# Stick-breaking attention with weights and values in two parts, both parts of the values in one stationary operand, a PSUM bank a head

## The chip, the core and the metric

The kernel runs on one core of a Trainium2 chip. A core has five engines that work side by side and follow one another through semaphores: TensorE (PE: the matmuls; PEld is its loading of stationary operands), VectorE (DVE), ScalarE (ACT), GpSimd (POOL) and SyncE (SP, which issues transfers). The metric is the device time of one execution in microseconds (us); lower is better.

## The reference, cut to what matters

Two transformer blocks run one after the other on one sequence of 512 positions with 1024 features, in fp32. The second block mixes three attentions, and the change is in one of them, stick-breaking attention, which has 8 heads of 64 features:

```
z = einsum('bqhd,bkhd->bhqk', q_b, bk) * HEAD_DIM ** -0.5
causal = kpos[None, :] < qpos[:, None]
log_beta = log_sigmoid(z)
log_one_minus = where(causal, log_sigmoid(-z), 0.0)
tail = cumsum(log_one_minus, reverse=True) - log_one_minus
a = where(causal, exp(log_beta + tail), 0.0)
return einsum('bhqk,bkhd->bqhd', a, bv)
```

Its result goes through a matrix (`@ w_up_b`) and is weighted with a gate, `merged = gates_a * ya + gates_b * yb + gates_c * yc`, where each gate is the sigmoid of a projection with a bias.

## The kernel before, in words

All activations lie with the features on the 128 partitions and the 512 positions along the free dimension. The large matrix products are made in fp32r, a format in which one pass does not carry all of fp32's digits; so each operand is held as a high and a low part, and each product takes three matmuls (high by high, low by high, high by low). Weights come by DMA as fp32; ACT rounds them to the high part `whi` (L358) and DVE subtracts to get the low part `wlo` (L359). The main matmuls (L231) accumulate one tile of 128 features by 512 positions in one of three PSUM banks, named `pd`; an evacuation on DVE or ACT frees the bank.

Small work runs as Python generators beside that stream. `start(gen, rate)` hangs a generator in, and after every so many main matmuls `pump` lets it take a step; `finish(gen)` runs what is left of it at once. The order in each engine's queue is then set by priorities when the program is built. A generator of stages goes through `pipeline`: in step i it issues stage 0 of unit i, stage 1 of unit i-1 and stage 2 of unit i-2.

Stick-breaking attention is the generator `stick`. It has 32 units: a pair of heads c = 0 to 3, a block of 128 keys kt = 3, 2, 1, 0, and a head hh = 0, 1 of the pair. Since a query sees only earlier keys, a unit has N = 512 - 128 kt queries: 128, 256, 384 and 512 columns. A unit does:
- stage 0: q·k into a PSUM bank `ps` of four (L584, L585), a mask by a small matmul (L1152), then on ACT abs (L180), exp and log(1 + x) (both L177), on DVE the softplus (L1158), which for kt < 3 is split in parts `P` by ACT (L547) and DVE (L548);
- stage 1: the running sums are added into `ps` by matmuls with triangular and all-ones matrices (L1169 in fp32 at kt = 3, L1172, L1177), while POOL keeps the sums of the key blocks passed so far (L1182 to L1190); ACT then takes the exponential of `ps` into a tile `PT` (L177), one of five such tiles;
- stage 2: the weights times the values. When the second head of a block comes to it, two fp32 matmuls (L1206) are issued, one a head, each with 64 stationary columns, for the upper and the lower 64 partitions of one bank `po`. That bank was cleared by a matmul with zeros at the pair's start (L1200), and ACT copies it out at the pair's end (L1210). The profile shows each fp32 matmul of L1206 as two instructions.

q·k and the triangular matmuls are made at least 256 columns wide or, at kt = 3, in fp32.

Beside `stick` runs `gated`, for the gate and the matrix of memory attention: for each half, four gate tiles (evacuated to `H` by DVE, L749), then one group of four sigmoids on ACT (`act_group`, L186, with a load of the activation tables ahead of it and another ahead of the next exponential), then four tiles of the matrix, whose evacuation multiplies with the sigmoids (DVE, L763). Then `finish(g_sb)` ends `stick`, and the next stage makes tiles of keys and queries in turn (evacuations L1670 and L1631 on DVE). At the start of `stick`, the top-256 search of another attention (`topk`, L1078 and L1079) still runs on DVE.

```python
        self.start(g_sb, 2.8)
        merged = self.t("H16", [P, KD, S])
        bg = lambda b: (lambda j: 8 * b + j)
        self.gated("gc", "uc", bg(2), u, R, yc, merged, True)
        self.finish(g_sb)
```

Of the kernel before, what the change touches and what calls it, by code (L numbers as in the profile page):

```python
# [8 lines left out]
F32 = mybir.dt.float32  # L9
F32R = mybir.dt.float32r  # L10
BF16 = mybir.dt.bfloat16
AF = mybir.ActivationFunctionType
# [5 lines left out]
P = 128  # L18
S = 512
D = 1024  # L20
KD = D // P
NT = S // P
# [115 lines left out]
NPT = 5  # L138
# [8 lines left out]
class Build:  # L147
# [82 lines left out]
    def mm(self, *args, **kw):  # L230
        return self.pe(self.nc.tensor.matmul(*args, **kw))  # L231
# [163 lines left out]
    def fm_tile(self, ws, rhs_hi, rhs_lo, cols):  # L395
        N = cols.stop - cols.start
        ps = self.bk_d()[:, 0:N]
        mm = self.mm
        for k, (hi, lo) in enumerate(ws):
            xh, xl = rhs_hi(k)[:, cols], rhs_lo(k)[:, cols]  # L400
            mm(ps, hi, xh, start=(k == 0), stop=False)
            mm(ps, hi, xl, start=False, stop=False)
            mm(ps, lo, xh, start=False, stop=(k == len(ws) - 1))
            self.pump(N / 4096.0)
        return ps

    def fm(self, name, rhs_hi, rhs_lo, evac, N=S):

        ps = self.fm_tile(self.next_half(name), rhs_hi, rhs_lo, slice(0, N))
        self.done_tile(lambda: evac(ps))  # L410
# [33 lines left out]
    def seven(self, name, x, pairs, evac):  # L444

        nc = self.nc

        def product(ps, b, start=False):  # L450
            hi, lo = x[b]
            kw = dict(skip_group_check=True)
            for k, (wh, wl) in enumerate(self.next_half(name)):
                self.mm(ps, wh, hi(k), start=start and k == 0, stop=False, **kw)
                self.mm(ps, wh, lo(k), start=False, stop=False, **kw)
                self.mm(ps, wl, hi(k), start=False, stop=k == 3, **kw)

        def head(q):
            q["g0"], q["c0"] = self.bk_s()[:, 0:256], self.bk_d()[:, 0:256]
            q["g1"] = self.seeded[:, 256 * (q["j"] % 2):256 * (q["j"] % 2) + 256]  # L460
            q["u2"], q["u4"] = self.t("s7", [P, 256], F32, bufs=2), self.t("s7b", [P, 256], F32, bufs=1)
            product(q["g0"], "11", True)

        def seed(q):
            nc.scalar.copy(q["g1"], q["g0"])

        def mid(q):
            product(q["c0"], "t3", True)
            product(q["g1"], "t2")
            nc.scalar.copy(q["u2"], q["g1"])  # L470
            product(q["g0"], "21")
            product(q["g1"], "t1")
            nc.scalar.copy(q["u4"], q["g1"])
            q["lin"] = self.tmp()
            nc.vector.tensor_add(q["lin"][:, 256:512], q["u4"], q["c0"])

        def tail(q, between):
            product(q["g1"], "22")
            between()
            gate = evac[0](q["g0"], q["g1"])  # L480
            product(q["c0"], "t4")
            nc.vector.tensor_add(q["lin"][:, 0:256], q["u2"], q["c0"])  # L482
            evac[1](q["j"], gate, q["lin"])
            self.done_tile(lambda: None)

        self.strict = "start"
        last = None
        for j in pairs:
            q = dict(j=j)
            head(q)  # L490
            if last is None:
                seed(q)
            else:
                tail(last, lambda: seed(q))
            mid(q)
            last = q
        if last is not None:
            tail(last, lambda: None)
        self.strict = None
# [284 lines left out]

    def softmax_finish(self, Pt, sums, N):
        nc = self.nc
        r = self.sm(1)
        nc.vector.reciprocal(r, sums)
        nc.vector.tensor_scalar(Pt[:, :N], Pt[:, :N], r, None, op0=ALU.mult)
# [348 lines left out]
    def stick(self, bk, bqh, bql, bv, y):  # L1138
        nc = self.nc
        units = [dict(c=c, kt=kt, hh=hh) for c in range(4) for kt in (3, 2, 1, 0) for hh in range(2)]  # L1140
        A, Ah, Al, o = {}, {}, {}, {}
        low = self.t("M4", [P, 2, 384], F32R)

        def s0(u):
            c, kt, h = u["c"], u["kt"], 2 * u["c"] + u["hh"]
            N = S - P * kt
            W = max(N, 256)
            z = self.bk_s()
            self.qk(z[:, :W], bk(h)[:, kt * P:(kt + 1) * P], bqh(h)[:, S - W:], bql(h)[:, S - W:])
            z = u["z"] = z[:, W - N:]  # L1150

            nc.tensor.matmul(z[:, :P], self.identb, self.strictb, start=False, stop=True, skip_group_check=True)  # L1152
            sp = u["sp"] = self.tmp()
            a = sp[:, :N]
            self.act(a, z[:, :N], AF.Abs)
            self.act(a, a, AF.Exp, scale=-1.0)
            self.act(a, a, AF.Ln, bias=self.ones[:, 0:1])
            nc.vector.scalar_tensor_tensor(a, z[:, :N], 0.0, a, op0=ALU.max, op1=ALU.add)  # L1158
            if kt < 3:
                hi = u["hi"] = self.t("P", [P, S], F32R, bufs=5)  # L1160
                lo = u["lo"] = self.t("P", [P, S], F32R, bufs=5)
                self.split_to(hi[:, :N], lo[:, :N], a)

        def s1(u):
            c, kt, h = u["c"], u["kt"], 2 * u["c"] + u["hh"]
            N = S - P * kt
            z, sp = u["z"], u["sp"]
            if kt == 3:
                nc.tensor.matmul(z[:, :N], self.ntri, sp[:, :N], start=False, stop=True, skip_group_check=True)  # L1169
            else:  # L1170
                for part in (u["hi"], u["lo"]):
                    nc.tensor.matmul(z[:, :N], self.ntrir, part[:, :N], start=False, stop=True,  # L1172
                                     skip_group_check=True)
                n = N - P
                parts = [Ah[h][:, 0:n], Al[h][:, 0:n]] if kt < 2 else [A[h][:, 3 * P:]]
                for part in parts:
                    nc.tensor.matmul(z[:, P:N], self.nones if kt < 2 else self.nones.bitcast(F32), part,  # L1177
                                     start=False, stop=True, skip_group_check=True)
            if kt == 3:
                A[h] = self.t("A", [P, S], F32, bufs=2)  # L1180
            if kt > 0:
                nc.gpsimd.tensor_copy(A[h][:, kt * P:(kt + 1) * P], sp[:, :P])  # L1182
                if kt < 3:
                    r = A[h][:, (kt + 1) * P:]
                    nc.gpsimd.tensor_add(r, r, sp[:, P:N])
                    Ah[h] = self.t("T", [P, S], F32R, bufs=2)
                    Al[h] = low[:, u["hh"], :]
                    a = A[h][:, kt * P:]
                    nc.gpsimd.tensor_copy(Ah[h][:, 0:N], a)
                    nc.gpsimd.tensor_sub(Al[h][:, 0:N], a, Ah[h][:, 0:N].bitcast(F32))  # L1190
            a = u["a"] = self.t("PT", [P, S], F32, bufs=NPT)
            self.act(a[:, :N], z[:, :N], AF.Exp)

        def s2(u):
            c, kt = u["c"], u["kt"]
            if u["hh"] == 0:
                return
            if kt == 3:
                o[c] = self.bk_o()
                nc.tensor.matmul(o[c], self.zb, self.zb[:, None, :].to_broadcast([P, 4, P]),  # L1200
                                 start=True, stop=True)
            us = [units[units.index(u) - 1], u]
            N = S - P * kt
            for hh in range(2):
                h = 2 * c + hh
                nc.tensor.matmul(o[c][64 * hh:64 * hh + 64, kt * P:], bv[:, kt, h * 64:(h + 1) * 64],  # L1206
                                 us[hh]["a"][:, :N], start=False, stop=True, skip_group_check=True)
            if kt == 0:
                y.append(self.t("Y", [P, S], F32, bufs=4))
                nc.scalar.copy(y[c], o[c])  # L1210

        yield from self.pipeline(units, [s0, s1, s2])

    def memattn(self, cq, mk, mv, y):
# [658 lines left out]
```

## Time and profile before

| | |
|---|---|
| time, median of 3 runs | 1727.21 us (1726.84 to 1728.08) |
| the profiled execution's own time | 1726.64 us |
| its span in the trace | 1724.9 us |
| PE matmuls busy | 1696.0 us, 98% of the span |
| PE weight loads busy | 1459.9 us, 85% |
| DVE busy | 1197.8 us, 69% |
| ACT busy | 916.4 us, 53% |
| POOL busy | 180.1 us, 10% |

The profile was taken on one execution. "Busy" counts the time in which an engine has an instruction in work; PE's matmuls overlap one another, so that a matmul's cost on PE is read from the start of one to the start of the next, and not from its own duration.

### The profile page before, as it was taken

How to read it: one execution, taken by the hardware profiler on the slowest of the kernel's cores; microseconds unless marked ns; L12 is line 12 of the kernel's file. 1: busy time of each engine (PE TensorE's matmuls, PEld its weight loads, DVE VectorE, ACT ScalarE, POOL GpSimd, SP SyncE). 2: the span in 40 equal slices, each digit the busy share in tenths (PEclk: the TensorE clock that was granted, in tenths of full speed). 3: DMA queues.
4: the chain of work that ended last, by engine and by line, in shares of the span. 5: the costliest groups of instructions: out<-in, count | busy, mean ns of one | idle time of the engine just before them, and what ended most of it. 6: DMA issues, size and time to landing. Idle time of an engine off the chain costs nothing. (4 is left out here: it accounts for less than half of the span.)

```text
span 1724.9 us, 27517 instructions
## 1 busy us (share of the span) xinstructions
PE 1696.0 (98%) x10178; PEld 1459.9 (85%) x10178; DVE 1197.8 (69%) x2515; ACT 916.4 (53%) x1875; POOL 180.1 (10%) x235
## 2 busy tenths in 40 slices
PE   8999999999999999999999999999999989999997
PEld 8878788888998989988989776777779979898997
DVE  5887765657866858886599944766655776585865
ACT  5755565545643635664455567644445454463542
POOL 1400001000100101000000223100001500010101
PEclk9999999999999999999999999999999999999999
DMA  5433215442655736245224111423233635474622
GB/s 180 123 90 122 77 59 150 132 141 91 161 152 128 186 114 159 73 132 170 86 78 106 62 62 61 116 82 117 66 120 103 162 85 145 125 183 117 156 75 82
DMA packets 74887, 199.75 MB, mean 116 GB/s; under 512 B 8864, under 2 KB 11464, under 8 KB 74496
## 3 DMA queue, kind: packets, MB, share of 16 engines
q1 hardware_dynamic: 64064, 178.53, 33.7%
q0 software_dynamic: 10688, 19.47, 6.9%
q8 instruction: 80, 1.31, 0.3%
q14 instruction: 55, 0.45, 0.1%
HBM read 187.45 MB, written 6.84 MB: 113 GB/s over the span
## 5 line engine op out<-in xcount | busy, mean ns | idle before, releaser
L358 ACT CAST whi<-raw 128x512 fp32r<-128x512 f32 (+2 forms) x504 | 288.3, 580 | 410.2 <-PE pd L231 269.3
L359 DVE TENSOR_TENSOR wlo<-raw,whi 128x512 fp32r<-128x512 f32 (+2 forms) x504 | 324.9, 650 | 204.8 <-ACT whi L358 198.8
L231 PE MATMUL pd<-uh,whi 128*128 128x512 f32 (+1 forms) x776 | 305.1, 393 | 0.0
L231 PE MATMUL pd<-uh,wlo 128*128 128x512 f32 (+1 forms) x776 | 304.5, 392 | 0.0
L231 PE MATMUL pd<-ul,whi 128*128 128x512 f32 (+1 forms) x776 | 303.5, 391 | 0.0
L231 PEld LDWEIGHTS pd<-uh,wlo 128*128 128x128 f32 x776 | 145.8, 188 | 33.9 <-issue 3.3
L231 PEld LDWEIGHTS pd<-ul,whi 128*128 128x128 f32 x776 | 145.9, 188 | 30.1 <-issue 1.7
L231 PEld LDWEIGHTS pd<-uh,whi 128*128 128x128 f32 x776 | 145.9, 188 | 29.8 <-issue 2.2
L231 PE MATMUL pd<-Yl,whi 128*128 128x256 f32 (+1 forms) x340 | 114.3, 336 | 3.8 <-ACT Yl L434 3.8
L231 PE MATMUL pd<-Yh,whi 128*128 128x256 f32 (+1 forms) x340 | 114.3, 339 | 0.9 <-DVE H L763 0.9
L231 PE MATMUL pd<-Yh,wlo 128*128 128x256 f32 (+1 forms) x340 | 114.0, 335 | 0.0
L231 PE MATMUL pd<-Ba,whi 128*128 128x512 f32 (+1 forms) x240 | 91.8, 383 | 1.2 <-DVE tmp L482 1.2
L231 PE MATMUL pd<-Ba,wlo 128*128 128x512 f32 (+1 forms) x240 | 90.9, 379 | 0.0
L231 PE MATMUL pd<-Ca,whi 128*128 128x512 f32 (+1 forms) x240 | 90.8, 378 | 0.0
L231 PE MATMUL ps<-ul,whi 128*128 128x256 f32 x296 | 83.2, 281 | 0.0
L231 PE MATMUL ps<-uh,wlo 128*128 128x256 f32 x296 | 83.1, 281 | 0.0
L231 PE MATMUL ps<-uh,whi 128*128 128x256 f32 x296 | 83.0, 281 | 0.0
L231 PE MATMUL pd<-Cb,whi 128*128 128x512 f32 (+1 forms) x210 | 79.8, 380 | 0.0
L231 PE MATMUL pd<-Bb,wlo 128*128 128x512 f32 (+1 forms) x210 | 79.6, 379 | 0.0
L231 PE MATMUL pd<-Bb,whi 128*128 128x512 f32 (+1 forms) x210 | 77.8, 380 | 1.4 <-ACT Bb L547 1.4
L358 ACT CAST whi<-PT 128x512 fp32r<-128x512 f32 x74 | 46.0, 621 | 58.9 <-PE po L231 25.1
L231 PEld LDWEIGHTS pd<-Yl,whi 128*128 128x128 f32 x340 | 64.2, 189 | 10.5 <-ACT Yl L434 4.1
(531 smaller groups left out, 4338.8 us busy)
## 6 DMA issues: line engine op xcount, KB each, us to landing
raw<-in_wts SPq DMA_DIRECT2D x202, 512.0 KB, 3.6
PT<-in_wts SPq DMA_DIRECT2D x74, 256.0 KB, 3.8
PT<-in_wts POOLq DMA_DIRECT2D x74, 256.0 KB, 5.1
raw<-in_wts SPq DMA_DIRECT2D x32, 448.0 KB, 3.4
P<-in_wts SPq DMA_DIRECT2D x37, 256.0 KB, 3.5
raw<-in_wts SPq DMA_DIRECT2D x8, 520.0 KB, 3.5
tabd<-tab SPq DMA_DIRECT2D x8, 320.0 KB, 5.8
H<-in_xT SPq DMA_DIRECT2D x8, 256.0 KB, 5.8
```

The source lines that it names most:

```text
L231: return self.pe(self.nc.tensor.matmul(*args, **kw))
L358: self.nc.scalar.copy(hi, r)
L359: self.nc.vector.tensor_sub(lo, r, hi.bitcast(F32))
```

## The change

For each unit the weights are split in a high and a low part (DVE, L1203 and L1204), which takes three `PT` tiles where there was one. For each pair of heads a new function `values` splits the values likewise (ACT L1147, DVE L1148) and lays them out so that a head's 64 high and 64 low columns stand side by side, as 128 stationary columns. Stage 2 then issues two fp32r matmuls a unit (L1213), one for each part of the weights, in the unit's own step. Their result has the products with the high values on one half of the partitions and those with the low values on the other; head 0 has the bank `po`, head 1 takes a bank `ps`. The matmul with zeros is gone. At a pair's end each head's two halves are added: ACT copies one half to SBUF (L1220), and DVE adds the other (L1221). Two scratch tiles of another function take other buffers. Lines behind the edit move (L1158 is L1167 in the changed kernel, L1152 L1161, L1172 L1181, L1177 L1186, L1670 L1683, L1631 L1644).

```diff
@@ in seven(): head(q)
-            q["u2"], q["u4"] = self.t("s7", [P, 256], F32, bufs=2), self.t("s7b", [P, 256], F32, bufs=1)
+            q["u2"], q["u4"] = [self.t(tag, [P, 256]) for tag in (("sc2", "sc3")[q["j"] % 2], "sc1")]
@@ in stick()
+        def values(c):
+            d = dual[c] = self.t("D8", [P, NT, 4, 64], F32R)
+            v = bv[:, :, c * P:(c + 1) * P].rearrange("p t (i x) -> p t i x", i=2)
+            nc.scalar.copy(d[:, :, 0::3, :], v)
+            nc.vector.tensor_sub(d[:, :, 1:3, :], v, d[:, :, 0::3, :].bitcast(F32))
+
+        values(0)
...
-            a = u["a"] = self.t("PT", [P, S], F32, bufs=NPT)
-            self.act(a[:, :N], z[:, :N], AF.Exp)
+            a = self.t("PT", [P, S], F32, bufs=NPT)[:, :N]
+            hi, lo = [self.t("PT", [P, S], F32R, bufs=NPT)[:, :N] for _ in range(2)]
+            self.act(a, z[:, :N], AF.Exp)
+            nc.vector.tensor_copy(hi, a)
+            nc.vector.tensor_sub(lo, a, hi.bitcast(F32))
+            u["a"] = hi, lo
 
         def s2(u):
-            c, kt = u["c"], u["kt"]
-            if u["hh"] == 0:
+            c, kt, hh = u["c"], u["kt"], u["hh"]
+            if kt == 3:
+                o[hh] = self.bk_s() if hh else self.bk_o()
+            w = dual[c][:, kt, 2 * hh:2 * hh + 2, :]
+            for i, part in enumerate(u["a"]):
+                nc.tensor.matmul(o[hh][:, kt * P:], w, part, start=kt == 3 and i == 0, stop=True, skip_group_check=True)
+            if kt > 0:
                 return
-            if kt == 3:
-                o[c] = self.bk_o()
-                nc.tensor.matmul(o[c], self.zb, self.zb[:, None, :].to_broadcast([P, 4, P]),
-                                 start=True, stop=True)
-            us = [units[units.index(u) - 1], u]
-            N = S - P * kt
-            for hh in range(2):
-                h = 2 * c + hh
-                nc.tensor.matmul(o[c][64 * hh:64 * hh + 64, kt * P:], bv[:, kt, h * 64:(h + 1) * 64],
-                                 us[hh]["a"][:, :N], start=False, stop=True, skip_group_check=True)
-            if kt == 0:
+            if hh == 0:
                 y.append(self.t("Y", [P, S], F32, bufs=4))
-                nc.scalar.copy(y[c], o[c])
+            m, r = (slice(64, 128), slice(0, 64)) if hh else (slice(0, 64), slice(64, 128))
+            q = self.tmp()
+            nc.scalar.copy(q[m, :], o[hh][r, :])
+            nc.vector.tensor_add(y[c][m, :], o[hh][m, :], q[m, :])
+            if hh == 1 and c < 3:
+                values(c + 1)
```

The order of instructions on each engine is set when the program is built, and it moves at three places that matter below. On ACT, about the first sigmoid group, where pair 0 passes to pair 1 (`H` holds the gates, `tmp` the chain of abs, exp and log, `PT` the weights), there stood:

```order
L1210 COPY Y_10877<-po_10655 128x512
L180 ACTIVATE tmp_10895<-ps_10891 128x256
L177 ACTIVATE PT_10907<-ps_10861 128x128
L186 ACT_TABLE_LOAD
L186 ACTIVATE H_2200_10528<-H_2200_10528,vecs_65 128x512 x4
L169 ACT_TABLE_LOAD
L358 CAST whi_11065<-raw_11013 128x512
```

and in the changed kernel there stands on ACT:

```order
L1220 COPY tmp_10928<-ps_10673 64x512
L1147 CAST D_2303_10931<-K_2157_10240 128x4x2x64
L180 ACTIVATE tmp_10950<-ps_10946 128x256
L180 ACTIVATE tmp_11051<-ps_11047 128x256
L177 ACTIVATE PT_10962<-ps_10908 128x128
L186 ACT_TABLE_LOAD
L186 ACTIVATE H_2200_10528<-H_2200_10528,vecs_65 128x512 x2
L177 ACT_TABLE_LOAD
L177 ACTIVATE tmp_10950<-tmp_10950 128x256
L186 ACT_TABLE_LOAD
L186 ACTIVATE H_2200_10528<-H_2200_10528,vecs_65 128x512 x2
L169 ACT_TABLE_LOAD
```

The group of four sigmoids is cut in two by an exponential, and there are four table loads where there were two. On DVE, at the end of `stick` (`pd` is a tile of the next stage, `P` the parts of the softplus), there stood:

```order
L1158 SCALAR_TENSOR_TENSOR tmp_11690<-ps_11686,tmp_11690 128x384
L548 TENSOR_TENSOR P_11673<-tmp_11667,P_11672 128x384
L548 TENSOR_TENSOR P_11696<-tmp_11690,P_11695 128x384
L1670 TENSOR_TENSOR tmp_11828<-pd_11797,R_8710 128x512
L359 TENSOR_TENSOR wlo_12091<-raw_11970,whi_12090 128x512
L1631 TENSOR_TENSOR tmp_11881<-pd_11848,R_8710 128x512
L1158 SCALAR_TENSOR_TENSOR tmp_11716<-ps_11712,tmp_11716 128x512
```

and in the changed kernel there stands on DVE:

```order
L1203 CAST PT_11906<-PT_11905 128x384
L1204 TENSOR_TENSOR PT_11907<-PT_11905,PT_11906 128x384
L548 TENSOR_TENSOR P_11923<-tmp_11917,P_11922 128x512
L1203 CAST PT_11931<-PT_11930 128x512
L1204 TENSOR_TENSOR PT_11932<-PT_11930,PT_11931 128x512
L1203 CAST PT_11943<-PT_11942 128x512
L1204 TENSOR_TENSOR PT_11944<-PT_11942,PT_11943 128x512
L1683 TENSOR_TENSOR tmp_12020<-pd_11989,R_8710 128x512
L1221 TENSOR_TENSOR Y_11950<-po_11790,tmp_11951 64x512
L1644 TENSOR_TENSOR tmp_12073<-pd_12040,R_8710 128x512
```

The evacuations of the next stage's first tiles stood between the blocks of the last units, and now all stand behind the last split of the weights. On PE, among the last units of `stick`, tiles of the next stage (`pd`) stood between the units:

```order
L231 MATMUL pd_11897<-uh_8097,whi_11840 128x512
L231 MATMUL pd_11897<-ul_8098,whi_11840 128x512
L1206 MATMUL po_11659<-PT_11657,K_2157_10240 64x256
L584 MATMUL ps_11712<-Cb_9997,Bb_9493 128x512
L585 MATMUL ps_11712<-G_10004,Bb_9493 128x512
L1152 LDWEIGHTS identb_136
L1152 MATMUL ps_11712<-strictb_138,identb_136 128x128
L231 MATMUL pd_11897<-uh_8097,wlo_11841 128x512
L231 MATMUL pd_11897<-uh_8097,whi_11840 128x512
```

and in the changed kernel the last 39 PE instructions of `stick` stand without one of them between, ending so on PE:

```order
L1213 MATMUL ps_11821<-PT_11906,D_2513_11753 128x384
L1181 MATMUL ps_11913<-P_11922,ntrir_134 128x512
L1213 MATMUL ps_11821<-PT_11907,D_2513_11753 128x384
L1181 MATMUL ps_11913<-P_11923,ntrir_134 128x512
L1186 MATMUL ps_11913<-T_11902,nones_132 128x384
L1186 MATMUL ps_11913<-M_2204_10545,nones_132 128x384
L1213 MATMUL po_11790<-PT_11931,D_2513_11753 128x512
L1213 MATMUL po_11790<-PT_11932,D_2513_11753 128x512
L1213 MATMUL ps_11821<-PT_11943,D_2513_11753 128x512
L1213 MATMUL ps_11821<-PT_11944,D_2513_11753 128x512
L231 MATMUL pd_12172<-uh_8097,whi_12081 128x512
```

There the next main tile, `pd_12172`, comes behind all of `stick`. Such unbroken runs stand at three places of the changed order: 26 instructions where pair 0 passes to pair 1, 54 in pair 2 and these 39 in pair 3; the order before has one, of 38, in pair 1's last and pair 2's first units.

## Rows read from the trace of the kernel before

**Rows 1.** The page's first lines: span, busy time of each engine.
```profile
span 1724.9 us, 27517 instructions
...
PE 1696.0 (98%) x10178; PEld 1459.9 (85%) x10178; DVE 1197.8 (69%) x2515; ACT 916.4 (53%) x1875; POOL 180.1 (10%) x235
```

**Rows 2.** By stretch: busy of PE, PEld, DVE, ACT, POOL; then DVE alone.
```profile
951.20:1103.50 152.30, 150.29 (x676) 105.91 (x675) 92.86 (x172) 101.11 (x217) 42.91 (x72) 1.00 0.20 64
...
954.10:988.90 34.80, 32.46 (x71) 1.00 0.12 38
```

**Rows 3.** All instructions of the line of the weights-times-values matmuls.
```profile
L1206 PE MATMUL po<-PT,K x64: 272/458/643, 963.7 to 1103.0; 128*64 128x128 f32 x16, 128*64 128x256 f32 x16, 128*64 128x384 f32 x16, 128*64 128x512 f32 x16
```

**Rows 4.** Timeline of PE about those matmuls: start, duration, line, operation.
```profile
963.72 0.43 PE L1206 MATMUL po<-PT,K 128*64 128x128 f32 x2
964.08 0.44 PE L584 MATMUL ps<-Ca,Ba 128*128 128x384 f32 x1
...
1032.10 0.39 PE L231 MATMUL pd<-ul,whi 128*128 128x512 f32 x1
1032.33 0.39 PE L231 MATMUL pd<-uh,wlo 128*128 128x512 f32 x1
1032.64 1.07 PE L1206 MATMUL po<-PT,K 128*64 128x512 f32 x2
1033.65 0.39 PE L584 MATMUL ps<-Cb,Bb 128*128 128x256 f32 x1
...
1041.67 0.38 PE L1200 MATMUL po<-zb 128*128 128x512 bf16 x1
1041.97 0.44 PE L1206 MATMUL po<-PT,K 128*64 128x128 f32 x4
1042.34 0.39 PE L1172 MATMUL ps<-P,ntrir 128*128 128x256 f32 x1
...
1045.68 0.28 PE L1172 MATMUL ps<-P,ntrir 128*128 128x256 f32 x1
1045.80 0.40 PE L231 MATMUL pd<-Yh,whi 128*128 128x512 f32 x1
...
1049.23 0.65 PE L1206 MATMUL po<-PT,K 128*64 128x256 f32 x2
1049.81 0.50 PE L584 MATMUL ps<-Cb,Bb 128*128 128x512 f32 x1
...
1093.82 0.87 PE L1206 MATMUL po<-PT,K 128*64 128x384 f32 x4
1094.61 0.50 PE L231 MATMUL pd<-uh,wlo 128*128 128x512 f32 x1
```

**Rows 5.** Groups on DVE in 955 to 1110: busy us, mean ns | idle before.
```profile
L548 DVE TENSOR_TENSOR P<-tmp,P 128x512 fp32r<-128x512 f32 x8 | 6.7, 843 | 1.0 <-ACT P L547 1.0
...
L1158 DVE SCALAR_TENSOR_TENSOR tmp<-ps,tmp 128x512 f32<-128x512 f32 x8 | 5.5, 688 | 9.1 <-ACT tmp L177 4.2 <-POOL M L1190 4.0 <-issue 0.9
...
L1158 DVE SCALAR_TENSOR_TENSOR tmp<-ps,tmp 128x128 f32<-128x128 f32 x7 | 2.0, 286 | 1.0 <-ACT tmp L177 0.9
...
L1081 DVE TENSOR_SCALAR sc<-sc 128x512 f32<-128x512 f32 x1 | 0.4, 417 | 0.0
```

**Rows 6.** PE's own waits in 940 to 1130: total, times, longest us.
```profile
PE pd L231 <- DVE H L763: 0.9, 1, 0.9
PE po L1206 <- ACT PT L177: 0.8, 1, 0.8
PE ps L1172 <- DVE P L548: 0.3, 1, 0.3
```

**Rows 7.** Timeline 1055 to 1060: the second sigmoid group, and what follows it.
```profile
1056.51 1.28 ACT L186 ACT_TABLE_LOAD   x1
...
1057.81 2.56 ACT L186 ACTIVATE H<-H,vecs 128x512 f32<-128x512 f32 x4
...
1059.31 0.50 PE L231 MATMUL pd<-Yh,whi 128*128 128x512 f32 x1 [0.90 <-DVE H L763]
```

More of the change, by code (lines that the diff above doesn't have):

```diff
@@ L1140, in stick @@
         units = [dict(c=c, kt=kt, hh=hh) for c in range(4) for kt in (3, 2, 1, 0) for hh in range(2)]
-        A, Ah, Al, o = {}, {}, {}, {}
+        A, Ah, Al, o, dual = {}, {}, {}, {}, {}
+        def values(c):
[4 more added lines that the diff above has]
+        values(0)
         low = self.t("M4", [P, 2, 384], F32R)
```

## The prediction, made before the changed kernel ran

> **What bounds the kernel now.** I read the page first: PE is busy for 1696.0 of 1724.9 us [rows 1], so the time is PE's work plus the little that PE waits. Next, the stretch of stick-breaking attention, 951.20 to 1103.50: PE 150.29 of 152.30 us, DVE 92.86, ACT 101.11, POOL 42.91 at a granted clock of 1.00 [rows 2]. So a microsecond of matmul removed here is a microsecond of time, as long as nothing makes PE wait longer; and DVE and ACT have a third of the stretch free on the mean. Means hide two things. In 954.10 to 988.90 DVE has no room: 32.46 of 34.80 us [rows 2], which is the top-256 search. And PE hardly waits because main matmuls stand between the steps of `stick` and cover its chains: its waits in the whole stage are one each of 0.9, 0.8 and 0.3 us, 2.0 in all [rows 6], all in the one place where no main matmuls stand between. So the questions are what the new matmuls save, and whether the cover lasts.
>
> **PE's saving.** A matmul's price is the distance from its start to the next start. Before, the line has 64 instructions, 16 of each width [rows 3], two to a matmul, so 8 matmuls of each. One head's matmul takes 963.72 to 964.08 = 0.36 at 128 columns, 0.58 at 256 (1049.23 to 1049.81) and 1.01 at 512 (1032.64 to 1033.65); both heads one behind the other (x4 in the rows) take 1041.97 to 1042.34 = 0.37 at 128 and 0.79 at 384 columns (1093.82 to 1094.61) [rows 4]. So two heads back to back cost as much as one: their column halves run together. The timeline shows 28 such groups, from 963.72 on, and four of them are x4: of the 16 pairs three at 128 columns and one at 384 stand together, the other 12 apart. A single 384 is taken at the pair's price, as at 128, so the sum is 5 x 0.36 + 8 x 0.58 + 7 x 0.79 + 8 x 1.01 = 20.1 us. Ahead of such a group the preceding fp32r matmul takes 0.31 (1032.33 to 1032.64) where its like takes 0.23 (1032.10 to 1032.33) [rows 4]: 0.08 for 28 groups, 2.2 us. The zero matmuls took 0.30 with such a gap (1041.67 to 1041.97), so 0.22 without: 0.9 for four. Removed: 23.2 us.
>
> The Trainium skill, page "TensorEngine Tiling (Array Packing)", section "Key Properties", states that tiles operate independently and can load and multiply in parallel; this speaks against giving up two 64-column matmuls, and the x4 rows agree with it.
>
> Added are 64 fp32r matmuls with 128 stationary columns. At 512 columns 0.23; at 256 columns 0.12 (1045.68 to 1045.80) [rows 4]; 384 between them, 0.175. 16 of each: 8.4 us. No fp32r matmul of 128 columns is in the trace. It is at least half of the 256, 0.06, and at most like one of the two instructions of the fp32 matmul that it replaces, 0.18 (half of 0.36) with some start cost, 0.22. I take the middle, 0.14: 2.2 us (1.0 to 3.5). Added: 10.6. **Saving 12.6 us, 11.3 to 13.8.**
>
> **Work added on DVE and ACT.** DVE gets a subtraction a unit, priced as the softplus of the same width, 0.69 at 512 and 0.29 at 128 [rows 5], 0.55 and 0.42 between: 8 x 1.95 = 15.6 us. It gets a copy a unit; none is in the trace. Bounds for 512 columns are 0.417, one input tensor, and 0.843, two input tensors while POOL works [rows 5]; a copy has one input, so I take 0.42, in the proportions of the subtractions 9.5 us, up to 19. Four value splits and eight additions of 0.69: 8.3. DVE goes from 92.9 to some 126 (up to 136) of 152 us, ACT from 101.1 to about 110 with four value casts, eight half copies for four whole ones and two more table loads of 1.28 [rows 7]. Both still fit on the mean and cost nothing where main matmuls cover them; what they cost is settled in three places where the changed order has none.
>
> **Pair 0 to pair 1 (26 PE instructions without a main matmul).** Up to there pair 0's units put 8 subtractions and copies on DVE: 2 x (0.69 + 0.55 + 0.42 + 0.29) = 3.9, copies 2.4, the values 0.7, 7 us; DVE has 34.80 - 32.46 = 2.3 free and may run 1 us into the next work: late by about 3.8, and PE waits at `P` and `PT`, behind which the main tiles stand in its queue. Then ACT does a copy, the value cast, two abs and an exponential (together about 2.0, an estimate from 0.64 for 512 columns), a table load of 1.28, the first sigmoids of 0.64 (2.56 for four [rows 7]) and DVE a product of 0.69 before the next tile's bank is free: 4.6, with 1.3 of PE work beside it, 3.3. The second load, which cuts the sigmoid group in two, delays the exponentials that the next splits need by 1.3. Together 8.4.
>
> **Pair 2 (54 instructions).** At the prices above PE's work is 54 x 0.175 = 9.5 (most are of 256 to 512 columns). ACT has four units in it, each with abs, exp, log and high part ahead of the triangular matmuls: 4 x 0.64 = 2.6 at 512 columns, 2.1 at 384 (0.55 / 0.69 of it), so 9.4; the hops from engine to engine add about 2.5 (0.9, 0.8 and 0.3 [rows 6] and one more of 0.5), and from the table load to the first matmul behind the sigmoids it is 56.51 to 59.31 = 2.8 [rows 7]. 14.7 - 9.5 = 5.2, of which 2.0 is there before [rows 6]: 3.2 more, plus copy and subtraction of the weights, 1.1, which now stand in the chain: 4.3.
>
> **The end of `stick` (39 instructions).** All three banks of the main tiles hold tiles of keys and queries whose evacuation stands on DVE behind the last subtraction, so PE has nothing to go on with. ACT's chain from the last 384-column units: 2.1 + 2 x 2.6 + 0.6 for the last exponential = 7.9, hops 2.4, DVE copy, subtraction, evacuation 0.42 + 0.69 + 0.69 = 1.8: 12.1. PE's work in it is 39 x 0.175 = 6.8. PE waits 5.3, in place of next to nothing, since main matmuls stood between before.
>
> **Sum.** 8.4 + 4.3 + 5.3 = 18.0 of new waiting, less 12.6: 5.4 us. Against the profiled execution, 1726.64 + 5.4 = 1732.0; the median lies 0.6 above it, so 1732.6, say **1732**. The three waits are added as if each chain went without overlap, so 18 is nearer their upper bound (22 with the dear copy); the lower is what the engines' spare time leaves, about 3.
>
> **Rivals.** *Faster*: priorities are static, but banks and buffers may let DVE and ACT run ahead before the three places, so that the chains start early. Then the waits come to some 3 us and the time to 1727.2 - 12.6 + 3 = 1718. For it: a third of DVE and ACT free [rows 2], and a zone of 38 instructions before that costs only 2.0 [rows 6]. Against it: the last zone has both ends fixed, by banks that are all held. It decides below waits of 9 us. *No change*: two of the three places cost as I say and the third nothing, 18 - 6 = 12 against 12.6: 1727. *Slower still*: POOL makes DVE's subtractions 0.84 instead of 0.69 [rows 5], which in the first zone adds 1 us and in the others 0.3 each, and the copies cost as much as the subtractions: 1738. *The halves run together anyway*: had the two heads' matmuls overlapped in all 16 pairs, the old price would be 4 x (0.36 + 0.58 + 0.79 + 1.01) = 11.0 rather than 20.1, the saving 3.5, and the time 1727.2 + 18 - 3.5 = 1742. The rows speak against it: x2 stands 12 times with other matmuls between. By the section "Key Properties" of the Trainium skill's page "TensorEngine Tiling (Array Packing)" this is what the old form could have had; the trace shows it only in the x4 rows.
>
> **How the numbers follow.** Forecast (1728 to 1738) 0.40, slower still 0.07, halves together 0.03, no change 0.25, faster 0.25. A measurement tells about 0.2%, 3.5 us, from no change, so the forecast's lower edge falls in with "same": slower 0.46, same 0.28, faster 0.26. Range for 8 in 10: 1717 to 1740; the forecast's own is 1728 to 1738.
>
> **What would show it.** Right: PE's busy time in the stage lower by 11 to 14 us, gaps on PE of 3 us and more in each of the three places, released by DVE `PT`, ACT `H` and DVE `tmp` of the evacuation; DVE busy about 126 us. Wrong: no gap over 1 us at the end of `stick` (the chain ran ahead), or 128-column matmuls under 0.08, or copies on DVE well away from 0.42. The prediction fails most likely by the size of the waits, which come from an order and not from a trace.

## The result, and the profile after

The changed kernel took 1741.50 us (median of 4, 1739.13 to 1744.17) where the kernel before, on the same chip, took 1727.12: a ratio of 1.008, 95% interval 1.0065 to 1.0095. So it is slower by 14.4 us. The forecast was slower, 1732, range 1717 to 1740; the time lies above the range.

The page of the changed kernel, first the lines that answer to [rows 1], then TensorE's granted clock in 40 slices of the span (9 stands for 90% or more):

```profile
span 1742.3 us, 27607 instructions
...
PE 1703.6 (98%) x10174; PEld 1475.5 (85%) x10174; DVE 1230.7 (71%) x2591; ACT 926.7 (53%) x1885; POOL 179.7 (10%) x235
...
PEclk9999999999999999999999998899999999999999
```

PE is as full as before, in shares. The new thing is the two eights: the kernel before has a 9 in every slice. They fall in the stage of stick-breaking attention, and so does most of the loss: at the stage's first main matmul the two traces are 0.14 us apart, and over the stage (from one and the same main matmul at 953 us to another at 1285.5 before) the changed kernel needs 14.96 us more; another 2.6 come behind it and were not traced. The profiled execution is the longest of the four, 1744.17 us. Its mean granted clock is 0.984, that of the two at 1741.4 and 1741.6 is 0.986, and that of the shortest, 1739.13, is 0.988; so the clock loss read from it below is likely above that of the median. Busy time by window, the stage as a whole, before:

```profile
953.27:1285.52 332.25, 330.24 (x1579) 244.72 (x1578) 208.02 (x485) 188.72 (x416) 42.91 (x72) 1.00 0.27 84
```

and after (PE, PEld, DVE, ACT, POOL, then the granted clock):

```profile
953.13:1300.34 347.21, 336.50 (x1575) 258.96 (x1574) 241.81 (x563) 198.16 (x424) 42.44 (x72) 0.95 0.27 81
...
990.00:994.00 4.00, 2.39 (x12) 1.21 (x11) 4.00 (x10) 1.99 (x6) 0.00 (x0) 1.00 0.52 158
994.00:996.00 2.00, 1.50 (x6) 0.70 (x4) 1.95 (x6) 1.47 (x4) 0.29 (x1) 0.54 0.08 33
996.00:1000.00 4.00, 2.47 (x8) 2.00 (x9) 2.46 (x6) 3.95 (x7) 0.00 (x0) 0.50 0.00 0
1000.00:1004.00 4.00, 4.00 (x11) 3.04 (x10) 0.73 (x2) 3.94 (x6) 0.00 (x0) 0.50 0.02 4
1004.00:1008.00 4.00, 4.00 (x18) 3.23 (x17) 1.70 (x4) 3.99 (x9) 0.59 (x2) 0.95 0.01 2
...
1092.00:1096.00 4.00, 2.12 (x8) 1.06 (x8) 3.73 (x6) 3.95 (x8) 2.21 (x4) 1.00 0.27 108
1096.00:1100.00 4.00, 3.68 (x11) 2.28 (x10) 3.86 (x7) 2.03 (x4) 1.51 (x2) 0.57 0.23 70
1100.00:1104.00 4.00, 3.71 (x9) 2.10 (x8) 2.73 (x5) 2.83 (x4) 0.00 (x0) 0.50 0.25 66
1104.00:1108.00 4.00, 4.00 (x13) 3.18 (x12) 3.88 (x7) 3.85 (x8) 0.00 (x0) 0.65 0.32 71
```

Read the short windows in order. Where pair 0 passes to pair 1, PE is busy for only 2.39 of 4 us; then the clock falls to 0.50, the 1.2 GHz level, and stays there while PE is full again (1000 to 1004: 4.00 of 4 us busy, 11 matmuls where 18 ran in the 4 us behind it). The end of `stick` shows the same. By the Trainium skill, "TensorE: Matmul & The Clock Gate", section "What's actually happening", the clock is halved or not by how busy TensorE has been lately, and has two levels; the rows agree. What a matmul loses is seen on PE's timeline at the end of `stick`:

```profile
1104.80 0.63 PE L231 MATMUL pd<-uh,whi 128*128 128x512 f32 x1
1105.22 0.63 PE L231 MATMUL pd<-ul,whi 128*128 128x512 f32 x1
...
1107.12 0.40 PE L231 MATMUL pd<-uh,whi 128*128 128x512 f32 x1
1107.35 0.39 PE L231 MATMUL pd<-ul,whi 128*128 128x512 f32 x1
```

Start to start it is 0.42 us at half clock and 0.23 at full.

From slices of 1 us the stage can be split in three sums: idle time (the slice less PE's busy time), clock loss (busy time times 1 less the granted clock), and the rest, work at full clock. Short waits that a matmul's recorded duration covers count as work.

| us of the stage | before | after | change |
|---|---|---|---|
| work | 330.24 | 321.39 | -8.85 |
| idle | 2.01 | 10.74 | +8.73 |
| clock loss | 0.00 | 15.08 | +15.08 |
| total | 332.25 | 347.21 | +14.96 |

The changed kernel does less work, as it was meant to, and loses that to waiting; the loss to the clock, which is at half for 34 us, is larger by itself than either. The table is an account of what PE did. It does not say what each line would be worth alone: matmuls at half clock also fill time in which PE might otherwise have waited. PE's own waits in 930 to 1160, which answer to [rows 6] (total, times, longest us; the longest six):

```profile
PE ps L1213 <- DVE PT L1203: 1.9, 5, 0.5
PE ps L584 <- ACT PT L177: 1.7, 5, 0.6
PE po L1213 <- DVE PT L1204: 1.5, 2, 0.8
PE ps L1181 <- DVE P L548: 1.3, 4, 0.5
PE pd L231 <- DVE H L763: 1.3, 2, 0.7
PE po L1213 <- DVE D L1148: 1.0, 1, 1.0
...
```

No wait is longer than 1.0 us, and no one of them is the cause: the splits of the weights, the score bank (a q·k that waits for an exponential to release a bank), the sigmoids and the values of the next pair each make a part.

### The profile page after: what moved, and what is told of

Same layout as the page of the kernel before. It is cut to its first block, busy times and chain, and to the rows that moved or that the text cites. A ratio compares the mean times of both kernels' runs of the same rounds, so it can differ in the third digit from the quotient of the medians.

```text
span 1742.3 us, 27607 instructions
## 1 busy us (share of the span) xinstructions
PE 1703.6 (98%) x10174; PEld 1475.5 (85%) x10174; DVE 1230.7 (71%) x2591; ACT 926.7 (53%) x1885; POOL 179.7 (10%) x235
```

## The experiments

For each run the text gives its time with that of the kernel before on the same chip, and the three sums of its stage. "Stage" is always the same thousand main matmuls.

**Theories.** A: head 1's bank is one of the four of the scores, and without it the steps fall behind the main matmuls. B: the splits on DVE are what PE waits for. And for the size of the loss: the half clock, or the waits themselves.

**The bank alone**, in the kernel before:

```diff
-                o[c] = self.bk_o()
-                nc.tensor.matmul(o[c], self.zb, ...)
+                o[0], o[1] = self.bk_o(), self.bk_s()
...
-                nc.tensor.matmul(o[c][64 * hh:64 * hh + 64, kt * P:], ..., start=False, ...)
+                nc.tensor.matmul(o[hh][64 * hh:64 * hh + 64, kt * P:], ..., start=kt == 3, ...)
...
-                nc.scalar.copy(y[c], o[c])
+                for hh in range(2):
+                    m = slice(64 * hh, 64 * hh + 64)
+                    nc.scalar.copy(y[c][m, :], o[hh][m, :])
```

> Of the change this keeps only that each head has its own bank, head 1 one of the four score banks; weights and values stay whole in fp32 with 64 stationary columns, and the matmul with zeros is gone. Theory A (the score bank that is given up lets main matmuls run out beside the steps, PE waits, and its clock halves): pair 2's run without main matmuls is 46 instructions instead of 38, so waits of 3 to 5 us more and 3 to 8 us at half clock, less 0.9 for the zero matmuls: 1731 to 1738 us. Theory B (the splits on DVE make the waits): 1726 to 1728. No theory has it faster than 1725.

1734.76 against 1726.81, ratio 1.0044 (1.0027 to 1.006). In the stage: work 330.20, idle 5.84, clock loss 0; 3.8 us more than before, all idle, the clock at 1.00 throughout. (Another 2.1 us of this profile stand ahead of the stage, where its clock is 0.83 in 230 to 240 and before's is 1.00, and 2.6 behind it.) With the bank come two half copies on ACT for each whole one; ACT's busy time in the stage is 4.7 us higher, so the bank is not quite alone. A's mechanism is there, without the half clock that I expected of it.

**The splits alone**, in the kernel before:

```diff
             self.act(a[:, :N], z[:, :N], AF.Exp)
+            hi, lo = [self.t("PT", [P, S], F32R, bufs=NPT)[:, :N] for _ in range(2)]
+            nc.vector.tensor_copy(hi, a[:, :N])
+            nc.vector.tensor_sub(lo, a[:, :N], hi.bitcast(F32))
```

> The kernel before with the copy and the subtraction of every unit added on DVE, in two more PT tiles that nobody reads; matmuls and banks as before. Theory A (the lost bank): the work fits beside, 1726 to 1730 us. Theory B (the splits on DVE are what PE waits for): 1733 to 1742, with the clock falling in the stage.

1731.27 against 1726.81, ratio 1.0025 (1.0014 to 1.0035). Work 333.26, idle 2.19, clock loss 0. By the medians 4.5 us, in the stage of the profiled execution (the shortest of its eight) 3.2, hardly any of it idle time and none clock loss: between what A and B expected, and too little for B.

**The matmuls without the splits** of the weights:

```diff
-            a = self.t("PT", [P, S], F32, bufs=NPT)[:, :N]
-            hi, lo = [self.t("PT", [P, S], F32R, bufs=NPT)[:, :N] for _ in range(2)]
-            self.act(a, z[:, :N], AF.Exp)
-            nc.vector.tensor_copy(hi, a)
-            nc.vector.tensor_sub(lo, a, hi.bitcast(F32))
-            u["a"] = hi, lo
+            hi = self.t("PT", [P, S], F32R, bufs=NPT)[:, :N]
+            self.act(hi, z[:, :N], AF.Exp)
+            u["a"] = hi, hi
```

> The changed kernel without the split of the weights: the exponential writes the high part itself, and both matmuls of a unit take it, so the low part is left out of the result; matmuls, banks, value splits and the two halves' sum are as in the changed kernel. Theory A (the lost bank): runs of 52 and 37 instructions without a main matmul remain, so of the 12.6 us saved only some are seen: 1722 to 1732 us, with the clock falling once or twice. Theory B (DVE's splits): the saving is seen whole, 1714 to 1718.

The low part is left out, and the high part is multiplied twice. 1735.16 against 1726.81, ratio 1.0053 (1.0037 to 1.0069): slower than before with 12 us less work and no split of weights, above what either theory expected. Work 318.11, idle 12.20, clock loss 9.52. B falls as the main cause. And a bank that alone cost 3.8 us stands here beside a loss of 20.

**Repeated q·k products** in the uncovered places of the changed kernel:

```diff
-            self.qk(z[:, :W], ...)
+            more = 2 if (c, kt) in ((0, 0), (1, 3), (2, 2), (2, 1), (2, 0), (3, 3), (3, 1), (3, 0)) else 0
+            for _ in range(1 + more):
+                self.qk(z[:, :W], ...)
```

> The changed kernel with the q.k products of the units in the three places without main matmuls made three times over, each overwriting the same scores: 64 more fp32r matmuls, about 11 us of work if none of it lay in waits. If most of the loss is the halved clock, the work keeps the clock at 1.00 longer and the time falls under the changed kernel's 1741.5: 1730 to 1738. If the loss is the waits alone, it stays or grows: 1741 to 1752.

1743.77 against 1726.81, ratio 1.0099 (1.0084 to 1.0114): no faster. Work 331.01, idle 11.20, clock loss 6.32. The clock loss fell by 8.8 us, and the added work of 9.6 ate it. The products stand at the head of the chain, so they may also have made each chain later; that was not traced. By its time the run speaks against the clock, by its sums for it; a better-placed run stands further below.

**Gate tiles first**: the eight gate tiles and two sigmoid groups ahead of the eight tiles of the matrix (weights ordered alike), for the changed kernel and for the kernel before:

```diff
+        if gname == "gc":
+            for j in range(8):
+                self.fm(gname, ..., lambda ps, j=j: ev_gate(ps, j))
         for g in range(2):
-            for j in range(4 * g, 4 * g + 4):
+            for j in range(4 * g, 4 * g + 4) if gname != "gc" else ():
```

> The changed kernel with the eight gate tiles and their two groups of sigmoids ahead of all eight tiles of the matrix, where four of each stood in turn. Its order has no run of 20 or more instructions of stick without a main matmul. Cover theory (the loss comes from PE standing uncovered, first waiting, then at half clock): the clock stays at 1.00 in the stage and the change's saving shows: 1712 to 1719 us. Rival (the added work on DVE, or the dearer steps themselves, cost the time wherever they stand): 1730 or more.

> The kernel before with the same order of gate tiles and matrix tiles. It loses its one uncovered run of 38 instructions, in which PE waited for 2.0 us: 1723 to 1727 us by either theory. What the changed kernel's twin is below this one is what the change is worth when it is covered: cover theory 8 to 13 us, rival nothing or a loss.

Both expectations say something wrong of the orders: the changed kernel so ordered still has runs of 37 and 87 instructions without a main matmul, and its twin one of 26. So the first doesn't test the cover. It took 1742.34 against 1727.72, ratio 1.0078 (1.0061 to 1.0095): work 320.30, idle 13.25, clock loss 10.72, idle time and clock loss of 24.0 together (25.8 in the changed kernel) in other places. The twin took 1724.46, ratio 0.9986 (0.9977 to 0.9995), with 0.66 us idle. In a covered order the kernel before gets faster; the changed one cannot be covered this way.

**Pairs**: the kernel before, its two heads' matmuls forced to stand together:

```diff
-            for hh in range(2):
+            r = None
+            for hh in (1, 0):
...
+                with ExitStack() as order:
+                    if r is not None:
+                        order.enter_context(self.tc.issue_after(r.ins))
+                    r = nc.tensor.matmul(o[c][64 * hh:64 * hh + 64, kt * P:], ...)
```

> The kernel before with the second head's matmul of a block issued first and the first head's ordered behind it, so that all 16 pairs stand back to back; nothing else is changed and no work is added. If the two column halves run together whenever they stand together, the pairs cost 11.0 us instead of 20.1, and 12 gaps of 0.08 go: 10 us less, 1716 to 1720. If the pairs in the uncovered run save nothing, or the later start of the first head's matmul makes a bank late: 1721 to 1726. If the overlap seen in the x4 rows is only how they are recorded: 1727.

1720.01 against 1727.72, ratio 0.9955 (0.9941 to 0.997). Work 319.16, idle 3.11, clock loss 1.65. All 16 pairs show as x4 in the timeline, the dearest like this:

```profile
990.10 1.08 PE L1210 MATMUL po<-PT,K 128*64 128x512 f32 x4
991.11 0.49 PE L231 MATMUL pd<-Yh,whi 128*128 128x512 f32 x1
```

1.01 us for two heads, as much as for one in [rows 4]. The 11.1 us of work saved are no less than the changed kernel's, with no work added on DVE or ACT and no bank taken; 2.8 us come back as idle and clock loss, in the one run without main matmuls.

**Pairs and gate tiles first** together:

> The paired kernel with the gate tiles ahead of the matrix tiles. Cover theory: both gains add, 1712 to 1717 us; if the pairing is worth nothing, as the kernel before with the same order of tiles, 1723 to 1727.

1714.23 against 1727.72, ratio 0.9925 (0.991 to 0.994): work 317.66, idle 0.97, clock loss 0. The gains more than add: 3.3 us for the order and 7.7 for the pairs make 11.0. With the rate of `stick` at 2.6 instead of 2.8:

> The paired kernel with the gate tiles first and the rate of stick at 2.6 instead of 2.8, which leaves no run of 20 instructions without a main matmul, where the one at 2.8 has one of 21 and 1.0 us of idle PE: 1712 to 1715 us, within 1.5 us of that one either way.

1714.51 against 1728.45, ratio 0.9921 (0.9906 to 0.9936), idle 0.38: the same time. These two are 13.5 and 13.9 us faster than before and 27 faster than the changed kernel.

**Zeros in the waits** of the changed kernel, ahead of the instructions that wait:

```diff
+        def zeros(u, out, n):
+            if (u["c"], u["kt"]) in ((0, 1), (0, 0), (2, 2), (2, 1), (2, 0), (3, 1), (3, 0)):
+                b = out.shape[1] // P
+                for _ in range(n):
+                    nc.tensor.matmul(out, self.zb, ..., start=False, stop=True, skip_group_check=True)
...
+                zeros(u, z[:, :N], 2)
                 for part in (u["hi"], u["lo"]):
...
             for i, part in enumerate(u["a"]):
+                zeros(u, o[hh][:, kt * P:], 1)
```

> The changed kernel with 56 matmuls that add zeros (bf16, 256 to 512 columns, some 11 us of work) in the units of the three uncovered places, ahead of the triangular matmuls and of the products with the values, where PE waits, so that the chain on the other engines is not made longer. The changed kernel's stage against before: 8.9 us less work, 8.7 us more idle PE, 15.1 us lost to the half clock. If the half clock comes from PE's idling and is most of the loss, the zeros take it to under 6 us and the idle time to under 7: 1731 to 1739 us, faster than the changed kernel although work is added. If the clock does not answer to it: 1745 to 1753.

1737.78 (1737.04 to 1738.72) against 1728.45, ratio 1.0056 (1.0041 to 1.0071); the changed kernel's four runs lie above all of these, though the two intervals touch. Work 329.74, idle 8.88, clock loss 4.62. PE got 8.3 us more to do and the stage became 4.0 us shorter, since the half clock went from 34 us to 10. Its stage, which answers to the changed kernel's 347.21, is:

```profile
954.13:1297.36 343.23, 334.32 (x1631) 257.41 (x1630) 241.39 (x563) 194.35 (x422) 43.01 (x72) 0.99 0.27 82
```

The place where it held best is the end of `stick`; the run's windows there, beside the 1096 to 1104 at 0.57 and 0.50 above, are:

```profile
1090.00:1100.00 10.00, 8.42 (x42) 4.87 (x41) 8.69 (x13) 7.41 (x15) 6.08 (x9) 1.00 0.18 52
1100.00:1110.00 10.00, 9.26 (x38) 6.43 (x37) 8.67 (x15) 8.77 (x14) 0.00 (x0) 1.00 0.43 110
```

Idle time stayed over the 7 us that I had set. That the clock is a loss of its own, on top of the waits, is shown by this run, but not for all of its size: 10.5 us of clock loss and 1.9 of idle time went, 8.3 of zeros took their place, and 4.0 came out as time. Whether the rest would have been waits at full clock is not shown.

**Less work, nothing else**: the kernel before with each product of weights and values cut to 8 columns:

```diff
-                nc.tensor.matmul(o[c][64 * hh:64 * hh + 64, kt * P:], ..., us[hh]["a"][:, :N], ...)
+                nc.tensor.matmul(o[c][64 * hh:64 * hh + 64, kt * P:kt * P + 8], ..., us[hh]["a"][:, :8], ...)
```

> The kernel before with each product of weights and values cut to 8 columns, so that most of it is left out: some 20 us less work on PE in the same places, nothing added on any engine and no bank taken. If work saved on PE is time saved: 1705 to 1709. If the part saved in the uncovered run becomes waiting there, and then half clock: 1709 to 1717, with more idle time than the 2.0 us of before and the clock falling in that run.

1719.33 against 1728.45, ratio 0.9953 (0.9936 to 0.9969). Work 318.06: 12.2 us less, not the 20 that I had taken, so short products cost more than their columns: one of 8 columns that stands alone takes 0.21 us from its start to the next matmul's (962.80 to 963.01). Idle 3.72, clock loss 1.58: of 12.2 us saved, 3.3 came back in the uncovered run. The time lies above both of the ranges that I gave.

**Head 1's bank from the main tiles**, in the changed kernel:

```diff
-                o[hh] = self.bk_s() if hh else self.bk_o()
+                o[hh] = self.bk_d() if hh else self.bk_o()
```

> The changed kernel with head 1's bank taken from the three of the main tiles instead of the four of the scores. If the score bank that was given up is what lets the steps fall behind: idle time under 6 us, clock loss under 6, 1722 to 1733. If it is the longer chain through ACT and DVE (splits, values, sums), or if any lost bank costs as much: 1737 to 1748.

1740.40 against 1728.45, ratio 1.007 (1.0055 to 1.0085). Work 319.98, idle 16.36, clock loss 9.62. A in its narrow form, that it is a bank of the scores, falls. The run does not tell whether any lost bank costs as much or whether it is the longer chain through ACT and DVE; the expectation has the same time for both.

**Less work and the bank**, without splits, value parts or sums; to the run without values comes this, and as in the run of the bank alone two half copies on ACT for each whole one (ACT's busy time is 2.4 us higher, PE has four zero matmuls more):

```diff
-                o[c] = self.bk_o()
-                nc.tensor.matmul(o[c], self.zb, ...)
+                o[0], o[1] = self.bk_o(), self.bk_s()
+                for b in (o[0], o[1]):
+                    nc.tensor.matmul(b, self.zb, ...)
```

> The kernel before with each product of weights and values cut to 8 columns (most of it left out, as in the run without values, 1719.3 us) and head 1 in a score bank of its own; both banks are cleared by a matmul with zeros, four more of them, 0.9 us. If the lost bank is what makes saved PE work into waiting and half clock: 1729 to 1737, near the 1735.2 of the changed kernel without weight splits. If the bank costs here only what it cost alone, 3.8 us in the stage: 1722 to 1726.

1727.17 against 1727.98, ratio 0.9996 (0.9987 to 1.0005). Work 318.45, idle 4.93, clock loss 8.13. Windows of 10 us about pair 2 in the run without values:

```profile
1040.00:1050.00 10.00, 8.00 (x36) 5.41 (x35) 3.83 (x6) 7.30 (x15) 5.65 (x8) 0.83 0.28 93
1050.00:1060.00 10.00, 8.77 (x42) 6.77 (x42) 5.94 (x12) 9.96 (x20) 0.56 (x2) 1.00 0.06 7
```

and with the bank taken:

```profile
1040.00:1050.00 10.00, 8.04 (x37) 5.41 (x35) 4.71 (x9) 8.54 (x21) 5.43 (x12) 0.81 0.18 54
1050.00:1060.00 10.00, 9.20 (x27) 5.93 (x27) 4.24 (x7) 8.69 (x15) 3.37 (x5) 0.50 0.01 2
```

The same PE work, hardly more idle time (1.2 us), and 6.6 us more of clock loss: with PE's work cut, the bank that cost 3.8 us of waiting costs 8.1 in the stage, and most of it is the clock, which stays at 0.50 for all of 1050 to 1060. The time lies between my two ranges: above that of a bank that costs what it cost alone, below the 1729 of the bank as the whole cause.

**Values split once**, in the run of the matmuls without the splits (pair 0's values are used for all pairs):

```diff
+            if c:
+                dual[c] = dual[0]
+                return
             d = dual[c] = self.t("D8", [P, NT, 4, 64], F32R)
```

> The run without weight splits (1735.2 us; its result leaves the low part out) with the values of pair 0 split once and used for all pairs, so that three casts on ACT, three subtractions on DVE and the wait of 1.2 us for them go. If these stand in the chain from pair to pair and bring down the clock: 1723 to 1730. If the bank and the sums decide: 1732 to 1736.

1733.90 against 1727.98, ratio 1.0028 (1.0018 to 1.0038). Work 316.44, idle 10.97, clock loss 12.07. The sums are those of the longest of its ten executions, 1737.37 at a mean clock of 0.984; the shortest took 1729.58 at 0.990. By the ratios the value splits are worth some 4 us (1.0028 after 1.0053, with intervals that touch), by the medians 2.4, and are not what decides.

## Why the prediction was wrong, step by step

- **PE's saving, 12.6 us.** The saving is there: 12.1 us less work without the weight splits, 8.9 with them. PE's recorded busy time, which was to fall by 11 to 14, rose by 6.3, since matmuls at half clock last longer. The 128-column matmul, for which I took 0.14, costs from 0.06 to 0.14 in the twelve that ran at full clock, 0.10 on the mean; the cheapest is like this, the second row 0.06 behind the first,

```profile
964.64 0.22 PE L1213 MATMUL po<-PT,D 128*128 128x128 f32 x1
964.70 0.44 PE L231 MATMUL pd<-uh,whi 128*128 128x512 f32 x1
```

  so by prices alone it would have been 13.2. The 3 us between the two figures of work go with the weight splits and not with the new matmuls: the splits alone, beside the old matmuls, added 3.0. Short waits that count as work are the likely part; they were not traced.
- **Work on DVE, 33.4 us.** 241.81 - 208.02 = 33.8. That the total fits is in part luck. The copy of 512 columns took 0.421, as taken, but the one of 384 took 0.767 on the mean where I had 0.33, and the subtraction of 384 took 0.730 where I had 0.55; against this, neighbours on DVE overlap by some 0.07 us, which I had not counted.
- **The three places.** Right, all three. Their idle time by windows of 10 us is 3.6 us (990 to 1000), 4.3 (1040 to 1070, of which 2.0 were there before) and 2.8 (1090 to 1110), where I had 8.4, 4.3 and 5.3 of new waiting: 8.7 us more than before in all, and not 18. I had added the chains without overlap and said so. With the clock loss of 4.1, 6.2 and 4.8 the three places cost 7.8, 8.5 and 7.6 us more than before. One of my signs of being wrong came: no wait at the end of `stick` is over 1 us. Nor does PE wait there for the evacuation of a main tile, which I had named. It waits for `P` and for the splits of the weights, longest in the first row, and the first main matmul behind them, in the second, starts without a wait:

```profile
1093.70 0.44 PE L1213 MATMUL po<-PT,D 128*128 128x384 f32 x1 [0.83 <-DVE PT L1204]
...
1103.35 0.79 PE L231 MATMUL pd<-uh,whi 128*128 128x512 f32 x1
```

- **The step that failed** is the sum, "18.0 of new waiting, less 12.6". It prices a wait at its own length, with the granted clock of 1.00 of [rows 2] carried over to an order with three uncovered places. The term that was missing is the half clock, 15.1 us in the profiled execution, more than all else: -8.9 + 8.7 + 15.1 = 14.9. That the total of 5.4 was only 9 off is errors that partly cancel: the waits came out 9.3 us below the sum, the saving 3.7 below it, and the clock 15.1 above.
- **The rival "faster"** needed waits below 9 us. It got them, 8.7 in all, and the kernel was still slower: the point from which it decides leaves out the clock too.
- **The bank** was in the diff and in none of my terms. With its two half copies it costs 3.8 us of waiting in the stage; together with shorter matmuls 8.1, waiting and clock.
- **The halves that run together.** I gave this rival 0.03, since 12 of 16 pairs stood apart, and as a description of the kernel before that was right. As a way to the same saving it is the better one: with all pairs together the kernel is 27 us faster than the changed one, when gate tiles come first.
- **The smaller rivals.** "No change" and "slower still" missed the clock too; the latter's price for subtractions beside POOL is met by the copies (below). "Slower still" at 1738 and "the halves run together" at 1742 lie nearest to 1741.5 by number, and that is luck: neither has the clock, and the latter needs a saving of 3.5 that was at least 8.9.

What stays open: how the changed kernel's losses divide between bank, weight splits and pair sums. Each alone costs little (3.8 us in the stage for the bank, 3.2 for the splits). Beside less PE work, new idle time and clock loss come to 3.3 us with nothing else, 11.0 with the bank, 19.7 with bank, value parts and sums, and 23.8 in the changed kernel; and since the order of the whole stage moves with each, the parts don't add.

## What to carry to other kernels

Where PE is nearly always busy, a saving is time only where other matmuls stand ready to take its place: look in the changed order for runs without them, and price each such run twice, for its waits and for the half clock behind them, which here took more of PE's time than the waits. Less PE work in a stretch that waits for other engines can bring the clock down: with the products cut to 8 columns, and nothing added, it fell where it had not before, and 3.3 of 12.2 us came back. Before giving up a bank and adding work for cheaper matmuls, see whether the old ones can be put side by side: two 64-column products back to back cost as much as one here, 1.01 us at 512 columns.

## What the runs showed of the hardware that was not expected

The clock fell without a long gap: from 990 to 994 the longest idle stretch of PE was 0.68 us, and PE was busy for 2.39 of the 4 us. And a copy on DVE is slower beside POOL: two copies of the same 384 columns in the changed kernel, one alone and one beside POOL's subtraction, in the timeline,

```profile
982.90 0.34 DVE L1203 CAST PT<-PT 128x384 fp32r<-128x384 f32 x1
...
1024.33 1.02 POOL L1199 TENSOR_TENSOR M<-A,T 128x384 fp32r<-128x384 f32 x1
1024.45 1.12 DVE L1203 CAST PT<-PT 128x384 fp32r<-128x384 f32 x1 [2.00 <-ACT PT L177]
```

take 0.34 and 1.12 us. The mean of the 384-column copies is 0.767, above the 0.421 of the 512-column ones, of which seven ran while POOL was idle and one beside a POOL copy. The Trainium skill, "GPSIMD Engine Reference", section "Specifications", says that the two engines share their way to SBUF; the rows agree.
